# Layer ends of a float32 transformer on one core: weights of the next layer split ahead into free slots, VectorE and ScalarE in program order up to the end of the next layer's first group

## The chip, the cores and the metric

The kernel runs on one core of one Trainium2 chip. The metric is the device time of one launch in microseconds; it counts as changed when it moves by more than the measurement can tell. All operands are float32 in memory and all weights lie in HBM.

## The reference, cut to what matters

A forward pass over 512 positions of width 1024, two blocks of four layers in all, each layer a mixer and a gated FFN with a residual around each:

```python
def rms_norm(x, g):  # x / sqrt(mean(x*x) + eps) * g, over the 1024 channels
def first_block(x, ...):
    for layer in range(DEPTH):              # 2: retention, then attention with a shared K and V
        if layer < N_A_LAYERS:
            h = retention(rms_norm(x, a_norm_pre[i]), a_w_in[i], a_w_out[i])
            x = x + rms_norm(h, a_norm_post[i])
        else:
            kv = rms_norm(x, kv_norm) @ w_kv
            h = diff_attention(rms_norm(x, b_norm_pre[i]), k_sh, v_sh, b_w_q[i], ...)
            x = x + rms_norm(h, b_norm_post[i])
        h = conv_ffn(rms_norm(x, ffn_norm_pre[layer]), ffn_w_up[layer], ...)
        x = x + rms_norm(h, ffn_norm_post[layer])
    return x
```

The second block is a conformer convolution, an FFN, NSA attention and an FFN, its residuals without a norm behind the branch.

What matters here: in the first block the branch's output is normed before it is added, so a layer cannot begin before the sums over all 1024 channels of the branch's output are known. There are four such layer ends: retention to FFN 0, FFN 0 to shared K and V ("diff"), attention to FFN 1, FFN 1 to conformer.

## The kernel before, in words

Activations lie transposed: a row tile is 128 channels by 512 positions, eight of them make x. Matmul operands are pairs of a rounded high part and a low part, and each product is three matmuls (high·high, high·low, low·high; mm3, L250 to L255). Weights stream in chunks of eight 128x128 tiles (Stream): SyncE loads a chunk into one of four raw buffers (L92), ScalarE writes its high part (L106) and VectorE its low part (L107) into one of three split buffers. A chunk's split buffer is free again when TensorE has passed the chunk that lay there. All weights are taken in the order in which the program is traced, so the position of a take in the program decides when its chunk is split.

A planner orders each engine's instructions by their place in the program and by when it takes their inputs to be ready. Where the program asks for a manual schedule for an engine (in_order), the instructions that it traces there keep their program order on that engine.

A layer's last columns are `tail` (L326): they are computed in two halves of 256 positions, each weight being used twice, so that the sums of squares of the first half (Residual.sums, L289 by colsum) can be taken while the second half is still multiplied. From the sums come the scale per position (L305, L306 and the Newton steps L296 to L299) and its spread over 128 channels by two transposes into a bank (L312). In done, L337 adds the column to the branch's output, L339 squares it, L341 adds the square to the sums. Only TensorE is kept in program order, during the tail.

The next layer begins with a group of six columns (`group`, L409): the banks of six columns are open at once and each row tile of x is multiplied into all six as soon as it is ready. In group_halves the first three row tiles are taken in halves (L457), then row tiles 3 to 7 in full (outer, L473 and L474 with the high part of x, L477 with the low part). A row tile is made by Residual.apply (L202 multiplies the branch by the spread scale, once a half; L204 adds it to x), then its high part on ScalarE (L267) and its low part on VectorE (L268). For the group's own norm each row tile of x is squared on ScalarE (L276 the first, L279 the others) and added on VectorE (L280); the norm's scale is not needed before the columns are read out of their banks, so its sums (L289), Newton steps and spread (L312) stand behind the group. Row tiles 3 to 7 and the norm are left to the planner. Outside the four layer ends the same group is used without a residual (Prep.step).

In ffn, six columns (three gated pairs) come from the group; gated reads a pair out of its banks (L661, L665), convolves (L640, L642) and makes the next operand (L667, L670, L264, L265). The columns of the fourth pair are traced behind the three pairs. In diff, a few small instructions for lambda (L843 to L852) are traced ahead of the group; pq (L267, L268 again) prepares a second norm of the same x behind it.

## Time and profile before

| | |
|---|---|
| median of 3 runs | 2697.86 us (2697.57 to 2698.37) |
| the profiled execution | 2698.97 us |
| its span, first to last instruction | 2697.2 us |
| TensorE matmul busy | 2663.1 us (99%) |
| VectorE busy | 1679.4 us (62%) |
| ScalarE busy | 1200.1 us (44%) |
| mean granted TensorE clock | 0.997 |

In the rows below, a row of a timeline gives the start in us from the span's start, the duration in us, engine, line, operation, what it writes and reads, and in square brackets the idle time of the engine before it and what ended it. A row with x18 stands for that many instructions in a row. PE is TensorE, DVE VectorE, ACT ScalarE. Ends of matmuls are modelled and overlap the next start; starts are what to compare.

### The profile page before, as it was taken

Reading aid. Unit: us, or ns where it says so; the run is one execution under the profiler, and the core shown is the slowest. Engines: PE = TensorE matmul, PEld = TensorE weight load, DVE = VectorE, ACT = ScalarE, POOL = GpSimd, SP = SyncE. Lnnn points to the kernel's source line nnn. Section 1 sums busy time; section 2 is a strip of 40 time slices with the busy share of each in tenths; the row PEclk is TensorE's granted clock in tenths of the full one; section 3 lists DMA queues with packets and bytes.
Section 4 is the critical chain, followed back from the end, with each engine's and each line's share of the span. In section 5 each row is a group of like instructions: output and inputs, shape, how many; then the busy total and the mean of one; then the engine's idle time right before and its main releaser. Section 6 shows DMA issues by size and latency. Waiting matters only on the chain.

```text
span 2697.2 us, 35698 instructions
## 1 busy us (share of the span) xinstructions
PE 2663.1 (99%) x14187; PEld 2223.9 (82%) x14187; DVE 1679.4 (62%) x2777; ACT 1200.1 (44%) x1956; POOL 118.8 (4%) x125
## 2 busy tenths in 40 slices
PE   9999999999999999999999999999999999999999
PEld 8888888788888878788888588888887777888887
DVE  6545557836656687845748966445447788564453
ACT  5443434434445674533434244323347676442331
POOL 0000000000001100000003300000001111000000
PEclk9999999999999999999999999999999999999999
DMA  5223222323322112322323323223343101223322
GB/s 181 79 75 101 82 79 71 109 94 97 101 86 87 57 46 78 94 94 99 99 90 105 111 72 96 98 94 119 117 136 122 40 9 44 75 94 95 101 95 86
DMA packets 73256, 243.46 MB, mean 90 GB/s; under 512 B 9216, under 2 KB 12160, under 8 KB 73088
## 3 DMA queue, kind: packets, MB, share of 16 engines
q1 hardware_dynamic: 73088, 241.18, 28.1%
q8 instruction: 111, 1.82, 0.3%
q14 instruction: 57, 0.47, 0.1%
HBM read 229.63 MB, written 4.19 MB: 87 GB/s over the span
## 4 chain that ended last, share of the span: by engine, by line
PE 89%; DVE 7%; ACT 2%; issue 1%; POOL 0%; DMA 0%; SPq 0%; POOLq 0%; ACTq 0%; DVEq 0%
PE bank L253 23%; PE bank L255 23%; PE bank L254 23%; PE bank L473 3%; PE bank L474 3%; PE bank L477 3%; PE bank L770 2%; PE bank L457 2%; DVE bank L1079 1%; PE bank L1559 1%; PE bank L826 1%; PE bank L1068 1%; PE bank L289 1%; DVE w_spl L107 1%; DVE arena_f L642 1%
## 5 line engine op out<-in xcount | busy, mean ns | idle before, releaser
L253 PE MATMUL bank<-arena_r,w_spl 128*128 128x512 f32 (+1 forms) x2732 | 1059.5, 388 | 4.8 <-ACT w_spl L106 2.6
L254 PE MATMUL bank<-arena_r,w_spl 128*128 128x512 f32 (+1 forms) x2732 | 1052.3, 385 | 0.8 <-DVE arena_r L265 0.8
L255 PE MATMUL bank<-arena_r,w_spl 128*128 128x512 f32 (+1 forms) x2732 | 1049.4, 384 | 0.8 <-DVE w_spl L107 0.8
L106 ACT ACTIVATE w_spl<-w_raw 128x1024 fp32r<-128x1024 f32 (+1 forms) x424 | 448.4, 1058 | 728.9 <-PE bank L254 456.0
L107 DVE TENSOR_TENSOR w_spl<-w_raw,w_spl 128x1024 fp32r<-128x1024 f32 (+1 forms) x414 | 507.3, 1226 | 401.6 <-ACT w_spl L106 398.6
L253 PEld LDWEIGHTS bank<-arena_r,w_spl 128*128 128x128 f32 x2732 | 514.4, 188 | 108.9 <-ACT w_spl L106 4.8
L255 PEld LDWEIGHTS bank<-arena_r,w_spl 128*128 128x128 f32 x2732 | 514.0, 188 | 102.6 <-DVE w_spl L107 1.6
L254 PEld LDWEIGHTS bank<-arena_r,w_spl 128*128 128x128 f32 x2732 | 514.3, 188 | 98.4 <-issue 1.4
L642 DVE SCALAR_TENSOR_TENSOR arena_f<-arena_f,vec 128x510 f32<-128x510 f32 (+1 forms) x264 | 194.9, 747 | 3.4
L264 ACT ACTIVATE arena_r<-arena_f 128x512 fp32r<-128x512 f32 (+1 forms) x153 | 91.9, 610 | 189.8 <-DVE arena_f L670 152.4
L253 PE MATMUL bank<-w_spl,arena_r 128*128 128x256 f32 (+1 forms) x480 | 138.9, 290 | 2.1 <-ACT arena_r L1346 1.5
L665 DVE TENSOR_TENSOR arena_f<-bank,arena_f 128x512 f32<-128x512 f32 x88 | 60.7, 689 | 125.9 <-PE bank L255 125.9
L473 PE MATMUL bank<-arena_r,w_spl 128*128 128x512 f32 (+1 forms) x350 | 136.2, 391 | 2.2 <-ACT arena_r L264 1.9
L255 PE MATMUL bank<-w_spl,arena_r 128*128 128x256 f32 (+1 forms) x480 | 136.7, 286 | 0.1
L254 PE MATMUL bank<-w_spl,arena_r 128*128 128x256 f32 (+1 forms) x480 | 136.4, 284 | 0.0
L474 PE MATMUL bank<-arena_r,w_spl 128*128 128x512 f32 (+1 forms) x350 | 135.7, 389 | 0.0
L265 DVE TENSOR_TENSOR arena_r<-arena_f,arena_r 128x512 fp32r<-128x512 f32 (+1 forms) x153 | 100.6, 670 | 35.2 <-ACT arena_r L264 34.5
L790 ACT ACTIVATE arena_f<-bank,small 128x128 f32<-128x128 f32 (+3 forms) x192 | 99.7, 526 | 49.5 <-DVE small L787 44.4
L667 ACT ACTIVATE arena_f<-arena_f 128x512 f32<-128x512 f32 x88 | 55.5, 631 | 138.6 <-DVE arena_f L642 138.5
L640 ACT ACTIVATE arena_f<-arena_f,vec 128x512 f32<-128x512 f32 x132 | 106.1, 809 | 19.5 <-DVE arena_f L661 17.6
L661 DVE TENSOR_TENSOR arena_f<-bank,arena_f 128x512 f32<-128x512 f32 x88 | 60.5, 688 | 81.3 <-PE bank L255 72.9
L787 DVE TENSOR_REDUCE small<-bank 128x1 f32<-128x128 f32 (+3 forms) x192 | 86.6, 483 | 23.2 <-PE bank L775 22.5
(228 smaller groups left out, 2894.0 us busy)
## 6 DMA issues: line engine op xcount, KB each, us to landing
w_raw<-w SPq DMA_DIRECT2D x422, 512.0 KB, 3.5
arena_f<-tab SPq DMA_DIRECT2D x10, 256.0 KB, 3.2
arena_f<-x SPq DMA_DIRECT2D x8, 256.0 KB, 6.4
x_wait<-arena_f SPq DMA_DIRECT2D x8, 256.0 KB, 2.1
arena_f<-x_wait SPq DMA_DIRECT2D x8, 256.0 KB, 2.6
out<-arena_f SPq DMA_DIRECT2D x8, 256.0 KB, 2.2
arena_r<-arena_f SPq DMA_DIRECT2D x20, 64.0 KB, 2.0
arena_r<-arena_f SPq DMA_DIRECT2D x20, 63.9 KB, 2.0
```

The costliest lines, as they stand in the source:

```text
L106: self.nc.scalar.activation(hi, r, AF.Copy)
L107: (self.lo_engine or self.nc.vector).tensor_tensor(lo, r, hi, op=ALU.subtract)
L253: mm(out, a[0], b[0], start=start, stop=False, skip_group_check=skip)
L254: mm(out, a[0], b[1], start=False, stop=False, skip_group_check=skip)
L255: mm(out, a[1], b[0], start=False, stop=stop, skip_group_check=skip)
L264: self.nc.scalar.activation(h, src, AF.Copy)
L265: self.nc.vector.tensor_tensor(l, src, h, op=ALU.subtract)
L473: mm(b, w[0], hi[:, sl], start=(k == 0 and sl.start == 0), stop=False, skip_group_check=True)
L474: mm(b, w[1], hi[:, sl], start=False, stop=False, skip_group_check=True)
L640: nc.scalar.activation(c.a, u.a, AF.Identity, bias=self.v(cb, j), scale=self.v(cw, 2 * nj + j))
L642: nc.vector.scalar_tensor_tensor(c.a[:, d:], u.a[:, :S - d], self.v(cw, (2 - d) * nj + j), c.a[:, d:], op0=ALU.mult, op1=ALU.add)
L790: nc.scalar.activation(p.a[:, :n], outs[c], AF.Exp, bias=mx[:, c:c + 1], accum_out=sm[:, c:c + 1])
```

## The change

Five things are changed, all around the four layer ends except the last two.

1. Stream can put the split parts of a chunk into a run of four free slots of the operand arena (parts with park, release). In the tail chunks are split up to three chunks beyond the tail's own weights, before its second half begins; nothing of them is taken back until the columns that use them have been passed.
2. From the tail's second half to the end of the next group VectorE and ScalarE are in program order, and TensorE from the tail's start to the end of the group. The order is written out: half_high and half_low, high, sums and low are traced one by one; the last column's done is traced between the first row tile's high and low part.
3. The group's norm: the sums (colsum) and the Newton steps are traced ahead of the last row tile's products, the spread right behind them. This holds for the groups without a residual too.
4. In ffn two columns of the fourth pair are traced between the first three gated pairs.
5. In diff the lambda instructions are traced behind the group.

```diff
-    def parts(self, upto):
-        while self.split < min(upto, self.n):
+    def parts(self, upto, park=False):
+        while self.split < min(upto, self.n) and (self.ring or park):
             c = self.split
+            if self.ring:
+                i = self.ring.popleft()
+                self.home[c] = (i, self.spl[:, i, 0], self.spl[:, i, 1])
+            else:
+                s = self.arena.run(4)
+                w = [self.whole[:, s[h].i:s[h].i + 2].rearrange("p a n -> p (a n)") for h in (0, 2)]
+                self.home[c] = (s, *w)
...
+    def high(self):
         b, k = self.b, len(self.xs)
         p = (b.R.get(), b.R.get())
         if self.update is not None:
             self.update.apply(k, slice(0, S))
-        b.pair(b.x[k].a, b.v(self.g, k), [s.a for s in p])
+        b.nc.scalar.activation(p[0].a, b.x[k].a, AF.Copy, scale=b.v(self.g, k))
         self.xs.append(p)
+    def low(self):
+        b, k = self.b, len(self.xs) - 1
+        hi, lo = self.xs[k]
+        b.nc.vector.scalar_tensor_tensor(lo.a, b.x[k].a, b.v(self.g, k), hi.a, op0=ALU.mult, op1=ALU.subtract)
         if self.want:
             self.squares.append(k)
+    def sums(self, n=KD):
+        while n > 0 and self.squares:
+            self.acc = self.b.sumsq(self.acc, self.b.x[self.squares.popleft()].a)
+            n -= 1
...
     def tail(self, name, ns, xs, ks, hs):
...
+        res.region = self.in_order(mybir.EngineType.PE)
+        res.region.__enter__()
+        W.holding = True
+        ahead = (len(W.order) + len(ns) * len(ks) - 1) // CHUNK + 4
...
+        for half, sl in enumerate(HALVES):
+            if half == 1:
+                W.parts(ahead, True)
+                res.order = self.in_order(mybir.EngineType.DVE, mybir.EngineType.Activation)
+                res.order.__enter__()
...
+                if half == 1 and n == ns[-1]:
+                    res.last = lambda: done(b, n, sl)
...
     def group(self, name, ns, prep):
...
-        for k in range(first, KD):
-            prep.step()
+        up = prep.update
+        if up is not None:
+            self.group_halves(name, list(ns), 3, banks, prep)
+        for k in range(max(0, len(xs) - 1), KD):
+            if up is None:
+                prep.step()
+            elif k < KD - 1:
+                prep.high()
+                prep.sums(2)
+                prep.low()
+            if k == KD - 1:
+                prep.sums()
+                st = self.P.get()
+                self.colsum(st, [prep.acc])
+                prep.acc.free()
+                rs = self.rstd(st.a, 4, D, True)
             self.outer(name, ns, k, banks, xs[k])
-        while prep.squares:
-            prep.acc = self.sumsq(prep.acc, self.x[prep.squares.popleft()].a)
-        return banks
+        if up is not None:
+            up.order.__exit__(None, None, None)
+            up.region.__exit__(None, None, None)
+        self.spread(st, rs)
+        rb = self.F.get()
+        self.nc.scalar.activation(rb.a, st.a, AF.Copy)
+        st.free()
+        return banks, rb, rs
     def group_halves(self, name, ns, m, banks, prep):
...
         for half, sl in enumerate(HALVES):
             for k in range(m):
-                prep.half(k, sl)
-                W.after = self.last_hi.ins
+                if k == 0:
+                    prep.half_high(0, sl)
+                    if half == 0:
+                        res.last()
+                        prep.half_low(0, sl)
+                        res.rest()
+                        prep.half_high(1, sl)
+                    else:
+                        prep.half_high(1, sl)
+                        prep.half_low(0, sl)
+                elif k == 1:
+                    prep.half_high(2, sl)
+                    prep.half_low(1, sl)
+                    if half == 0:
+                        prep.half_low(2, sl)
+                        res.scale(1)
+                elif half == 1:
+                    prep.half_low(2, sl)
+                if half == 1 and k > 0:
+                    W.release(ws[k, ns[0]][0])
+                    W.parts(ws[k, ns[0]][0] + NSPL)
...
-        W.hold()
+        prep.high()
+        prep.low()
+        W.go_on()
...
-                banks = self.group(up, ns, pr)
-                st, rs = self.norm_cols(pr.acc, keep=True)
+                banks, rb, _ = self.group(up, ns, pr)
+                nxt = []
                 for q in range(first):
                     ps.append(gated(banks[2 * q], banks[2 * q + 1], q))
-            elif j >= first:
+                    if q < 2:
+                        nxt.append(self.col(up, first + q * NF, xs))
+                ps.append(gated(*nxt, first))
+            elif j > first:
```

## Rows read from the trace of the kernel before

**Rows 1.** Page, part 1: busy us (share of the span) xinstructions.
```profile
PE 2663.1 (99%) x14187; PEld 2223.9 (82%) x14187; DVE 1679.4 (62%) x2777; ACT 1200.1 (44%) x1956; POOL 118.8 (4%) x125
```
**Rows 2.** Waits of TensorE: engine line, waited for: us, times, longest us.
```profile
PE bank L457 <- ACT arena_r L267: 5.8, 4, 1.4
PE bank L253 <- ACT w_spl L106: 3.1, 4, 0.9
PE bank L312 <- DVE small L299: 2.7, 3, 1.7
...
PE bank L312 <- DVE keep L299: 1.2, 2, 0.9
...
PE bank L477 <- DVE arena_r L268: 0.7, 1, 0.7
```
**Rows 3.** Timeline of TensorE where the shared K and V stage begins.
```profile
785.11 0.38 PE L312 MATMUL bank<-cst,small 128*128 128x128 f32 x2
...
785.91 0.28 PE L255 MATMUL bank<-arena_r,w_spl 128*128 128x256 f32 x1
787.64 2.42 PE L457 MATMUL bank<-arena_r,w_spl 128*128 128x256 f32 x18 [1.45 <-ACT arena_r L267]
789.90 0.95 PE L289 MATMUL bank<-vec,arena_f 128*128 128x1 f32 x8
790.71 0.84 PE L457 MATMUL bank<-arena_r,w_spl 128*128 128x256 f32 x5
```
**Rows 4.** Timeline of VectorE and of ScalarE at the same place.
```profile
785.52 0.75 DVE L202 TENSOR_TENSOR arena_f<-arena_f,bank 128x256 f32<-128x256 f32 x2
...
786.57 0.88 DVE L204 SCALAR_TENSOR_TENSOR arena_f<-arena_f,vec 128x256 f32<-128x256 f32 x2
...
787.08 0.51 ACT L267 ACTIVATE arena_r<-arena_f,vec 128x256 fp32r<-128x256 f32 x1
```
**Rows 5.** Timeline of TensorE at the end of retention.
```profile
415.39 0.43 PE L312 MATMUL bank<-cst,small 128*128 128x128 f32 x2 [0.55 <-DVE small L299]
```
**Rows 6.** VectorE by line and form, 793 to 817.5: xcount, busy us, mean ns, idle before.
```profile
L268 DVE SCALAR_TENSOR_TENSOR arena_r<-arena_f,vec,arena_r 128x512 fp32r<-128x512 f32 x10 | 7.2, 745 | 0.0
L107 DVE TENSOR_TENSOR w_spl<-w_raw,w_spl 128x1024 fp32r<-128x1024 f32 x4 | 4.9, 1222 | 0.4 <-ACT w_spl L106 0.4
L280 DVE TENSOR_TENSOR arena_f<-arena_f 128x512 f32<-128x512 f32 x7 | 4.8, 681 | 0.0
L204 DVE SCALAR_TENSOR_TENSOR arena_f<-arena_f,vec 128x512 f32<-128x512 f32 x5 | 3.7, 744 | 0.0
L202 DVE TENSOR_TENSOR arena_f<-arena_f,bank 128x256 f32<-128x256 f32 x9 | 3.5, 413 | 0.1
```
**Rows 7.** ScalarE by line and form in the same stretch.
```profile
L267 ACT ACTIVATE arena_r<-arena_f,vec 128x512 fp32r<-128x512 f32 x13 | 8.8, 709 | 0.0
L106 ACT ACTIVATE w_spl<-w_raw 128x1024 fp32r<-128x1024 f32 x5 | 5.3, 1060 | 4.9 <-issue 3.9 <-ACT arena_r L267 0.9
L279 ACT ACTIVATE arena_f<-arena_f 128x512 f32<-128x512 f32 x7 | 4.3, 616 | 0.0
```
**Rows 8.** Timeline of TensorE: first matmuls of two row tiles that follow each other.
```profile
801.79 0.40 PE L473 MATMUL bank<-arena_r,w_spl 128*128 128x512 f32 x1
...
805.89 0.39 PE L473 MATMUL bank<-arena_r,w_spl 128*128 128x512 f32 x1
```
**Rows 9.** Timeline of VectorE in the group of FFN 0.
```profile
444.52 1.23 DVE L107 TENSOR_TENSOR w_spl<-w_raw,w_spl 128x1024 fp32r<-128x1024 f32 x1 [0.71 <-ACT w_spl L106]
...
449.96 1.23 DVE L107 TENSOR_TENSOR w_spl<-w_raw,w_spl 128x1024 fp32r<-128x1024 f32 x1 [2.95 <-ACT w_spl L106]
```
**Rows 10.** Timelines of VectorE and TensorE behind the group of FFN 0.
```profile
472.72 1.22 DVE L107 TENSOR_TENSOR w_spl<-w_raw,w_spl 128x1024 fp32r<-128x1024 f32 x1
...
474.00 0.50 PE L255 MATMUL bank<-arena_r,w_spl 128*128 128x512 f32 x1 [0.38 <-DVE w_spl L107]
```
**Rows 11.** Stretch behind the end of retention: length, PE, PEld, DVE, ACT, POOL, PEclk, DMA, GB/s.
```profile
417.98:421.66 3.68, 3.68 (x19) 3.68 (x20) 2.94 (x6) 1.70 (x3) 0.00 (x0) 0.56 0.13 20
```

## What the change should do to the time, predicted from the trace of before

> **What bounds the kernel now.** I read the page's busy shares first: TensorE is busy for 99% of the span, so nearly everything that this change can win is idle time of TensorE, and anything that makes TensorE wait is lost in full, since nothing behind it has slack [rows 1]. Then the waits of TensorE, to see where the rest lies. The layer ends show up as L457, four times and 1.45 µs each, and L312 on "small", three times, of which the longest (1.7) belongs to a norm that the change does not touch; L477 and L312 on "keep" are in the conformer's group and, for 0.4 of its 1.2, the NSA group; L253 on "w_spl" is mostly weights that come late after the two first FFN groups [rows 2]. Then the timeline at a layer end (the shared-KV stage's): the two transposes that spread the first half's scale start at 785.11, call that moment S; the last matmul of the old layer starts at 785.91, and the first of the new one only at 787.64, so 1.6 µs are lost [rows 3], while VectorE does four instructions that the first row tile does not need between the two that it does [rows 4].
>
> **The switch itself.** In program order the chain from S is: L202 begins 0.41 later, 0.41 long, L204 0.48, L267 0.51, with hops of 0.03 to 0.05, so the first L457 can start at S+1.92 instead of S+2.53 [rows 3, 4]. That is 0.61 a layer end, 2.4 for four. The wait of L312 for the small scale [rows 5] comes from a weight split that VectorE runs ahead of it; in two ends it is 0.55 and 0.5. With the weights of three chunks split ahead into free slots during the last columns, VectorE has only half-width adds there (of L202's size, 0.41), nothing holds the scale up, and both waits go: 1.05, and 0.3 for the two restarts of the pipeline, 1.4. The splits moved ahead are three per end, 1.06 on ScalarE and 1.22 on VectorE each [rows 6, 7]; they lie beside old-layer columns in which VectorE is half idle, so I cost them at nothing; without that cover one of them would put back 1.2. Their loads on SP's queue go out earlier by the same three chunks, with four raw buffers still ahead; no wait of TensorE in the trace is on a load, so I cost this at nothing too, and at most one load (3.5 µs, the page's median) if it is not so.
>
> **What follows the switch.** Here is the cost. From the second half of the last columns to the end of the group VectorE and ScalarE now run exactly in program order. On the ruler S, TensorE needs, without waits, 1.92 + 6 × 2.16 for the six half row tiles (18 matmuls at 0.12, as 18 take 2.42 with the last one's drain) + 0.8 for L289 [rows 3] + 0.1 for L312 (an estimate: its pair's 0.38 less the drain) = S+15.8 until the first full row tile, and 4.10 for each of those (801.79 to 805.89) [rows 8]. It wants the sums of squares, now ahead of the last row tile, at S+15.8+4×4.10 = S+32.2.
>
> VectorE's queue: the second spread starts at S+7.05 (1.92 + 2×2.16 + 0.8), so the second halves begin 0.41 later; three half tiles are 3×1.19 (L202, L204, L268 in half width) and a wait of 0.5 for ScalarE, S+11.5. A weight chunk stands next: ScalarE's part ends at S+12.0, VectorE's at S+13.25. Row tile 3 is L202 twice, L204, wait for L267, L268: 0.34+0.45+0.75+0.74+0.75, so its high part is there at S+15.45 (in time for 15.8) and its low part at 16.2; behind another chunk's low part VectorE is free at S+17.6. From there a row tile is, in the order written (high, two sums, low, then the outer product's weight chunk): 0.34+0.45+0.75 for L202, L202, L204; then VectorE stands before its add until ScalarE has done L267 and the square behind it, 0.71+0.62 less the overlap, 1.30; the two adds 0.61 each, L268 0.67, the chunk's L107 1.15 (starts follow each other 0.08 closer than the durations in [rows 6, 7]). That makes 5.88 with two adds and 5.27 with one, against TensorE's 4.10. Row tile 4 has two squares to wait for (1.83 with L267), one add and no chunk: 4.65. Then 5.88, 5.88, 5.27 and a last add 0.65: 22.3, so the sums are done at about S+39.9 and not at 32.2. TensorE loses 7.7 a layer end, part of it on the way in row tiles 5 and 6, most of it before L289, and it stands there in program order with the whole last row tile behind it. Four ends: 30.8.
>
> That VectorE stands still with ready work behind it is seen before the change: at 444.52 it had waited 0.71 for ScalarE's half of a chunk, and the low part of a row tile and the last add came after it; but there the planner had spread the work so that the add was over at 447.0 and VectorE then idle for 2.95 [rows 9]. The Trainium skill (TensorE: Matmul & The Clock Gate, section "Architectural detail") says that ScalarE's and VectorE's queues are strict FIFO. By that rule the 7.7 stand; a queue that let ready work pass would leave the 1.2 of the rival below. The trace agrees with the rule in the row just named.
>
> **The other parts.** The norm's chain behind the group is hidden by the last row tile: 0.67 and 0.86 of idle in the conformer, with 0.3 of restarts 1.8; 0.4 in NSA [rows 2]. In the FFN groups it was already hidden by columns, so nothing there. After the two first FFN groups VectorE works off three gated pairs before the weights that stand behind them: the low part that TensorE waits for at 474.00 was split at 472.72 [rows 10]; with the hesitation around it and the 0.9 at 480.20 (a share of L253's 3.1 in [rows 2]) that is 2.1 a group. Two columns traced between the pairs bring their weight chunks forward, and the pairs no longer wait for the norm behind the group; the fourth pair is traced ahead of the next chunks, which takes some of it back. I take 1.5 of 2.1, twice 1.5 = 3.0; ends 0 and 4.2. The lambda block (six small VectorE and ScalarE instructions and one table load) goes behind the group; it was early and unneeded, nothing, at worst one load of a table. The groups without a residual only change the place of L289 and L312, whose inputs are ready long before: nothing.
>
> The clock: after the idle at 415.39 and 416.5 the granted clock of the next 3.68 µs was 0.56, that is mostly at 1.2 instead of 2.4 GHz, and the same 18 matmuls take 2.26 at 787.64 [rows 3, 5, 11]. Without the idle this 1.4 goes.
>
> **Sum.** −2.4 −1.4 −1.8 −0.4 −3.0 −1.4 + 30.8 = +20.4. The profiled execution took 2698.97 (span 2697.2); its sum is 2719.4. It lies 1.1 above the median 2697.86, so 2718.
>
> **Rivals.** *VectorE keeps pace* (faster). If its waits for ScalarE are filled, its own work from S+17.6 is 4×2.02 for the four row tiles, 7×0.61 adds, 3×1.15 chunks, 15.8: S+33.4, and TensorE loses 1.2 or, with any head start, nothing. Then the gains of 10.4 stand against 0 to 4.8: 2687 to 2692, say 2690. It decides itself where a row tile of VectorE takes 4.1. For it: the work was done in that time before [rows 9]. Against it: the written order. Chance 0.22.
> *Only the high part is waited for.* If the squares are done beforehand (0.6 less in four tiles) and the last chunk's low part falls behind the last add (1.15), the loss is 4.1 an end, 16.4 in all: +6, 2704. Chance 0.13.
> *Slower still.* Each layer end now has one idle of some 4.7 µs. If the clock falls after it as at 417.98, 1.4 is added once or twice an end: 2724 to 2729; other work that the planner lets into the region (eight row tiles of the second norm in the shared-KV stage, 0.67 of VectorE each) costs the same kind, up to 5. The Trainium skill (the same page, section "What's actually happening") says that an idle TensorE falls to half clock by itself. In this trace it did so after the idle at 415 and did not after the 1.45 at 787. Chance 0.12.
> *It does not do what it says:* should the region not hold VectorE and ScalarE to program order at all, the planner's order stays and with it the first rival's time; it is counted there.
>
> **How the numbers follow.** Forecast 0.53, 2711 to 2724; rivals 0.22, 0.13, 0.12. A measurement here tells 0.2%, 5.4 µs, from no change: faster is below 2692.5, slower above 2703.3. Faster 0.21; same 0.09 (the low side of the second rival and the top of the first); slower 0.70. The range goes from 2690, in the middle of the first rival, to 2728; about 0.15 is left out. The forecast's own range is 2711 to 2724, from the unknown share of the FFN weights and ±1.5 an end.
>
> **What would show it.** Right: at each layer end the first L457-like matmul 1.9 after the spread instead of 2.5; no wait for the small scale; then a wait of TensorE at the norm's sums of 4 to 5 µs, released by VectorE's add, and short waits on the row tiles' high and low parts in the two tiles before; VectorE's waits for ScalarE's squares some 1.3 each. Wrong: no wait at the sums, or one under 1.5; waits on weights in the parked slots or on loads, which would be a cause I have at nothing; or the FFN's waits for weights unchanged.

## The result and the profile after

The changed kernel takes 2723.39 us (median of four runs, 2721.82 to 2723.72), the kernel before 2698.11 (four runs, 2697.57 to 2698.91): ratio 1.0092, 95% interval 1.008 to 1.0104, so 25 us slower. The profiled execution took 2723.72 with a span of 2721.9.

First the page's busy line (busy us, share of the span, instructions), which answers to [rows 1]. The work is the same; TensorE has 8 us more busy time and 17 us more idle time.

```profile
PE 2671.1 (98%) x14187; PEld 2225.2 (82%) x14187; DVE 1685.0 (62%) x2777; ACT 1199.8 (44%) x1955; POOL 117.1 (4%) x125
```

Then the waits of TensorE (engine line, waited for: us in all, times, longest), the counterpart of [rows 2].

```profile
PE bank L575 <- DVE arena_r L210: 8.7, 7, 2.4
PE bank L302 <- DVE w_spl L118: 7.6, 2, 3.8
PE bank L571 <- ACT arena_r L203: 3.8, 8, 0.8
PE bank L555 <- ACT arena_r L188: 3.5, 4, 0.9
PE bank L300 <- ACT arena_f L503: 2.3, 3, 1.2
PE bank L300 <- DVE arena_f L1218: 2.0, 1, 2.0
```

L555 is the first half row tile (L457 before): 0.87 at each layer end instead of 1.45, as forecast. The wait for the small scale at two layer ends is gone. New are the waits of L575 for a row tile's low part (L210), of L571 for its high part (L203; one of the eight, 0.8, stands in the first group of retention), and two of 3.8 for a weight chunk's low part (L118). In none of the four layer-end groups is there a wait at the norm's column sums, L336.

Where the 25 us arise can be read off TensorE alone: both traces hold 14187 of its instructions, so the start of the n-th in one can be set against the n-th in the other. Where both have done the same work, the difference is the lag. (Worked out from the starts in the traces; columns of the table below: the time in the kernel before, and the lag of after.)

```
place                                            before    after
last columns of retention                         410.2     +1.0
first half row tile, FFN 0                        418.0     -0.4
first columns behind that group                   461.4     +2.4
behind the gated pairs of FFN 0                   492.6     +6.3
first half row tile, shared K and V               787.9     +5.7
behind that group                                 832.2    +13.3
first half row tile, FFN 1                       1048.1    +11.7
behind that group                                1089.5    +16.0
behind the gated pairs of FFN 1                  1116.8    +19.8
first half row tile, conformer                   1416.0    +19.2
behind that group                                1454.5    +23.8
behind its gated columns                         1467.6    +26.5
last instruction                                 2693.2    +24.7
```

The switches (from the last columns to the first half row tile) win 1.4, 0.6, 1.3 and 0.6; the lag ahead of the third is 13.0, and the two larger gains hold 0.7 each for the small scale's wait. The four groups lose 2.8, 7.6, 4.3 and 4.6, the first after winning 1.5 because the clock does not fall there. The stretches behind three of them lose another 3.9, 3.8 and 2.7.

The K and V group loses most. The planner put the low parts of the second norm of the same x (L210 again, eight of 0.75) into the ordered stretch, seven of them ahead of the last add, and a row tile of VectorE takes 6.58 there:

```profile
818.79 1.49 DVE L327 TENSOR_TENSOR arena_f<-arena_f 128x512 f32<-128x512 f32 x2 [1.31 <-ACT arena_f L326]
...
822.65 0.75 DVE L210 SCALAR_TENSOR_TENSOR arena_r<-arena_f,vec,arena_r 128x512 fp32r<-128x512 f32 x1
...
825.37 1.49 DVE L327 TENSOR_TENSOR arena_f<-arena_f 128x512 f32<-128x512 f32 x2 [1.31 <-ACT arena_f L326]
```

Both losses, in the group and behind it, have one place each in the timelines of FFN 0. TensorE first (start, length, line, operands, count, idle before and what ended it):

```profile
415.66 0.38 PE L359 MATMUL bank<-cst,small 128*128 128x128 f32 x2
...
417.61 0.61 PE L555 MATMUL bank<-arena_r 128*128 128x256 f32 x3 [0.87 <-ACT arena_r L188]
...
443.13 0.74 PE L575 MATMUL bank<-arena_r,w_spl 128*128 128x512 f32 x2 [1.51 <-DVE arena_r L210]
...
449.17 1.19 PE L575 MATMUL bank<-arena_r,w_spl 128*128 128x512 f32 x4 [0.60 <-DVE arena_r L210]
...
451.57 0.39 PE L300 MATMUL bank<-arena_r,w_spl 128*128 128x512 f32 x1
...
456.33 0.95 PE L336 MATMUL bank<-vec,arena_f 128*128 128x1 f32 x8
457.14 0.49 PE L571 MATMUL bank<-arena_r,w_spl 128*128 128x512 f32 x1
...
485.30 0.68 PE L302 MATMUL bank<-arena_r,w_spl 128*128 128x512 f32 x1 [3.81 <-DVE w_spl L118]
```

And VectorE at the same place:

```profile
440.92 1.49 DVE L327 TENSOR_TENSOR arena_f<-arena_f 128x512 f32<-128x512 f32 x2 [1.31 <-ACT arena_f L326]
...
446.96 1.49 DVE L327 TENSOR_TENSOR arena_f<-arena_f 128x512 f32<-128x512 f32 x2 [1.31 <-ACT arena_f L326]
...
455.42 0.69 DVE L327 TENSOR_TENSOR arena_f<-arena_f 128x512 f32<-128x512 f32 x1
...
463.85 0.68 DVE L754 TENSOR_TENSOR arena_f<-bank,arena_f 128x512 f32<-128x512 f32 x1
...
484.03 1.22 DVE L118 TENSOR_TENSOR w_spl<-w_raw,w_spl 128x1024 fp32r<-128x1024 f32 x1
```

VectorE stands 1.31 before its adds in row tiles 5 to 7, the tiles follow each other at 6.04 (440.92 to 446.96), and the last add ends at 456.11. With S at 415.66 that is S+40.4; the forecast had S+39.9. But TensorE does not stand there: from 451.57 to 456.33 it does 21 matmuls of the fourth pair's first column, which the planner put into the ordered stretch ahead of L336. What it loses it loses earlier, on low and high parts that come at VectorE's pace, and later: the late sums make the scale late, so the gated pairs start at 463.85 instead of 459.45 in the kernel before; VectorE works them off, the fourth among them, before it splits the chunk that TensorE needs next, and begins its low part at 484.03, with TensorE waiting.

The clock's side, in stretches (us; PE, PEld, DVE, ACT and POOL busy, instructions; granted clock; DMA share; GB/s). Behind FFN 0's switch it is at 2.4 GHz throughout, where [rows 11] showed 0.56. It fell to 1.2 GHz for most of some 3.5 us in four other places, each at the end of an idle of 2.0 to 3.8 us that the change had brought, or within 1.3 us of it.

```profile
415.60:450.00 34.40, 31.20 (x194) 26.93 (x194) 25.70 (x51) 13.85 (x23) 0.00 (x0) 1.00 0.16 47
...
485.30:488.90 3.60, 3.60 (x9) 2.84 (x10) 3.60 (x6) 1.22 (x2) 0.00 (x0) 0.53 0.58 181
1127.20:1130.70 3.50, 3.47 (x8) 2.77 (x9) 3.50 (x6) 1.10 (x2) 0.00 (x0) 0.52 0.61 171
1461.90:1465.10 3.20, 3.20 (x8) 2.55 (x9) 3.16 (x4) 0.00 (x0) 0.85 (x1) 0.50 0.06 20
1485.40:1489.20 3.80, 3.80 (x12) 2.95 (x11) 3.80 (x5) 2.37 (x4) 1.69 (x1) 0.55 0.69 177
```

### The profile page after: what moved, and what is told of

It reads as the page before. It is cut to its first block, busy times and chain, and to the rows that moved or that the text cites. A ratio compares the mean times of both kernels' runs of the same rounds, so it can differ in the third digit from the quotient of the medians.

```text
span 2721.9 us, 35688 instructions
## 1 busy us (share of the span) xinstructions
PE 2671.1 (98%) x14187; PEld 2225.2 (82%) x14187; DVE 1685.0 (62%) x2777; ACT 1199.8 (44%) x1955; POOL 117.1 (4%) x125
## 4 chain that ended last, share of the span: by engine, by line
PE 88%; DVE 7%; ACT 3%; issue 1%; POOL 0%; DMA 0%; SPq 0%; POOLq 0%; DVEq 0%; ACTq 0%
PE bank L300 24%; PE bank L302 24%; PE bank L301 24%; PE bank L575 2%; PE bank L571 2%; PE bank L572 2%; PE bank L862 2%; PE bank L1635 1%; PE bank L918 1%; DVE w_spl L118 1%; PE bank L1154 1%; PE bank L336 1%; DVE arena_f L251 1%; DVE bank L1165 1%; DVE arena_f L249 1%
## 5 line engine op out<-in xcount | busy, mean ns | idle before, releaser
L117 ACT ACTIVATE w_spl<-w_raw 128x1024 fp32r<-128x1024 f32 (+1 forms) x412 | 435.5, 1057 | 705.2 <-PE bank L301 446.8
L118 DVE TENSOR_TENSOR w_spl<-w_raw,w_spl 128x1024 fp32r<-128x1024 f32 (+1 forms) x402 | 493.1, 1227 | 373.3 <-ACT w_spl L117 370.0
L571 PE MATMUL bank<-arena_r,w_spl 128*128 128x512 f32 (+1 forms) x326 | 129.6, 399 | 6.0 <-ACT arena_r L203 3.2
```

What stands on the lines that cost most here:

```text
L117: self.nc.scalar.activation(hi, r, AF.Copy)
L118: (self.lo_engine or self.nc.vector).tensor_tensor(lo, r, hi, op=ALU.subtract)
L571: mm(b, w[0], hi[:, sl], start=(k == 0 and sl.start == 0), stop=False, skip_group_check=True)
```

## The experiments

Theory Q is the forecast's: VectorE and ScalarE, held to the written order through row tiles 3 to 7, set TensorE's pace and make the sums late. Its rivals: the columns moved between the gated pairs, the chunks parked ahead, or the place of the norm. All kernels below are the changed kernel with one edit, unless another base is named. Each was timed beside the kernel before, on the same chip. The table of lags at the end puts them side by side.

### Let the order go at the end of the half row tiles

```diff
         if up is not None:
-            up.order.__exit__(None, None, None)
             up.region.__exit__(None, None, None)
...
         prep.low()
         W.go_on()
+        res.order.__exit__(None, None, None)
```

> After, but VectorE and ScalarE leave program order at the end of the half row tiles; TensorE keeps it to the end of the group. By the count of TensorE's instructions the changed kernel falls behind by 3.7, 7.5, 4.3 and 4.4 us inside its four layer-end groups, 19.9 in all. Theory Q (the written order of VectorE and ScalarE in row tiles 3 to 7 is the cause): 14 to 20 of these come back, 2703 to 2709, and the 1.3 us waits of VectorE for squares go. Rival (the work itself, the weights split ahead or TensorE's order are the cause): within 3 us of 2723. The wait for a low part behind the FFN groups (3.98 and 3.82) stays at 2 to 4 by both.

Measured: 2693.27 (10 runs), ratio to before 0.998, interval 0.997 to 0.9989. That is 30 us below the changed kernel, more than all it had lost, and more than the 14 to 20 expected: the waits behind the FFN groups, which the expectation left at 2 to 4, went too. So both losses hang on the order of VectorE and ScalarE in row tiles 4 to 7 (row tile 3's high and low part are still written ahead of the place where the order is let go). With the waits went the clock's four new falls; one, at 866.91, came instead. One thing was given back. Timelines of ScalarE and TensorE at the end of retention:

```profile
415.91 1.06 ACT L117 ACTIVATE w_spl<-w_raw 128x1024 fp32r<-128x1024 f32 x1 [0.70 <-PE bank L301]
...
417.42 0.86 PE L555 MATMUL bank<-arena_r 128*128 128x256 f32 x5 [1.48 <-ACT arena_r L188]
```

A chunk that is traced behind the ordered stretch was placed in the middle of it, ScalarE's part ahead of the first half tile's high part, and the switch costs 1.48 again. The ordered stretch fixes the order of what is traced in it; it does not keep other work out.

### The norm behind the last row tile

```diff
-            if k == KD - 1:
-                prep.sums()
...
-                rs = self.rstd(st.a, 4, D, True)
             self.outer(name, ns, k, banks, xs[k])
+        prep.sums()
...
+        rs = self.rstd(st.a, 4, D, True)
```

> After, with the sums of squares, their column sums and the scale behind the last row tile again, in every group. The recorded forecast put most of the 7.7 us an end before the column sums, with the last row tile stuck behind them; by that, the last row tile (4.1) now covers more than half: 12 to 16 faster, 2707 to 2711. Theory F (columns of the next work that the planner put ahead of the column sums fill that wait already, and the loss is in the row tiles): within 4 us of 2723, rather slower by 0 to 3, as the conformer's and the NSA group's waits for the norm (0.7, 0.9 and 0.4 before) come back.

Measured: 2715.42, ratio 1.0061, 1.0046 to 1.0076: 8 faster than the changed kernel, between the two. The groups themselves lose 2.6, 6.7, 3.6 and 4.6, nearly as before; what goes is the loss behind the FFN groups, -0.2 each instead of +3.9 and +3.8, while 2.8 are lost between the conformer and the end, where after had won 1.8. TensorE's wait for the norm is back in the conformer's and the NSA group:

```profile
PE bank L359 <- DVE keep L346: 1.2, 2, 0.9
```

That covers 1.2 of these. Another 1.8 is a longer wait for the conformer's gated columns, 3.7 instead of 1.9 (the line is L1215 in after):

```profile
PE bank L300 <- DVE arena_f L1214: 3.7, 1, 3.7
```

VectorE behind FFN 0's group:

```profile
462.04 0.69 DVE L753 TENSOR_TENSOR arena_f<-bank,arena_f 128x512 f32<-128x512 f32 x1 [2.08 <-ACT arena_f L502]
...
480.50 1.22 DVE L118 TENSOR_TENSOR w_spl<-w_raw,w_spl 128x1024 fp32r<-128x1024 f32 x1
```

In the changed kernel the spread of the scale stands behind a last row tile that stands behind the late sums. With the last row tile in front, the spread and the pairs come 1.8 earlier (462.04 instead of 463.85), the late chunk 3.5 earlier. So the place of the sums costs, but not as the forecast had it: no wait at L336, but a late spread.

### The fourth pair's columns back behind the three pairs

```diff
-                nxt = []
                 for q in range(first):
                     ps.append(gated(banks[2 * q], banks[2 * q + 1], q))
-                    if q < 2:
-                        nxt.append(self.col(up, first + q * NF, xs))
-                ps.append(gated(*nxt, first))
-            elif j > first:
+            elif j >= first:
```

> After, with the fourth gated pair's columns traced behind the three pairs, as before the change (both FFN). Theory P (the fourth pair, traced ahead of the next chunk, makes the chunk's low part late): the two waits of 3.98 and 3.82 and the half clock behind each (1.9) go, 11.6, and the 1.85 that the columns brought forward had won comes back twice: 2715, 2712 to 2719. Rival (the pairs start 4.4 us late because the norm's sums are late, the place of the columns is not the cause): the waits stay above 2.5 each, 2720 to 2726.

Measured: 2719.28, ratio 1.0076, 1.0061 to 1.0091, 4 faster, just between the two ranges (2712 to 2719 and 2720 to 2726), half of the 8 expected. The wait for the chunk's low part, in the waits of TensorE of this run, has halved and not gone:

```profile
PE bank L302 <- DVE w_spl L118: 3.5, 2, 1.7
```

So the columns' place is about half of that wait, and the lateness of the pairs the other half. The next run shows which of them comes first.

### Order let go, and the columns back

Both edits above (the first and the third).

> Both edits of the two runs beside it: order released at the end of the half row tiles, and the fourth pair's columns back. If queue and columns are two separate causes, their gains add: 14 to 20 and 8, 2695 to 2702, near the kernel before. If the late sums cause both, the time is that of the release alone, within 2 us.

Measured: 2692.36, ratio 0.9978, 0.9969 to 0.9988: the time of the release alone, within 1. The gains do not add. With the sums in time the columns' place is worth nothing, for or against; the late sums cause both.

### Low part ahead of the sums

```diff
                 prep.high()
-                prep.sums(2)
                 prep.low()
+                prep.sums(2)
```

> After, with the low part of each row tile written ahead of the two sums instead of behind them; program order stays. Theory Q as counted in the forecast (VectorE's row tile is 5.9 us because it stands 1.3 before its adds): now it stands 0.7 before the low part and 0.5 before the adds, 1.2 in all, so the sums come hardly earlier, but each low part comes 1.9 earlier. TensorE's pace in the row tiles is still VectorE's: 2 to 6 faster, 2717 to 2721. Rival (only the lateness of the low part costs, 8.7 us of waits and their restarts): 9 to 14 faster, 2709 to 2714.

Measured: 2702.92, ratio 1.0015, 1.0006 to 1.0024: 20 us faster by moving one line, far outside both expectations. VectorE in FFN 0's group:

```profile
439.54 0.75 DVE L210 SCALAR_TENSOR_TENSOR arena_r<-arena_f,vec,arena_r 128x512 fp32r<-128x512 f32 x1 [0.79 <-ACT arena_r L203]
440.21 1.48 DVE L327 TENSOR_TENSOR arena_f<-arena_f 128x512 f32<-128x512 f32 x2
...
445.06 0.75 DVE L210 SCALAR_TENSOR_TENSOR arena_r<-arena_f,vec,arena_r 128x512 fp32r<-128x512 f32 x1 [0.79 <-ACT arena_r L203]
```

The row tile falls from 6.04 to 5.52 (439.54 to 445.06), because the squares now end while VectorE does the low part: one wait of 0.79 instead of 1.31. The expectation had two waits, 1.2 in all, and left out that the last square can be summed one tile earlier, ahead of the last chunk. So the sums end at 452.7, 3.4 before the changed kernel's, and that counts in the group and again behind the pairs: behind FFN 0's pairs this kernel loses nothing (-0.7 before and behind them in the table), the changed one 3.9. TensorE's waits for low parts (8.7 in the changed kernel) are gone too, those for high parts rise from 3.8 to 7.3, and of the clock's four new falls one is left, in FFN 1. What the earlier low parts are worth by themselves and what the earlier sums, this run does not separate.

### Adds one row tile behind their squares

```diff
                 prep.high()
-                prep.sums(2)
+                prep.adds()
                 prep.low()
+                prep.square(2)
             if k == KD - 1:
+                prep.adds()
                 prep.sums()
...
```

(`square` issues ScalarE's squares, `adds` VectorE's adds of the squares issued a tile earlier.)

> After, still in program order to the end of the group, but each add of a square is written one row tile behind its square: VectorE does the two halves, the step into x, the adds of the tile before, the low part, the chunk; ScalarE the high part, the squares, the chunk. Nothing then stands for ScalarE: a row tile is 1.54 + 1.22 + 0.67 + 1.15 = 4.6 us on VectorE against 4.1 on TensorE. Theory Q1 (the wait for the squares, as written, is what is too long; program order by itself is not): the row tiles lose 2 an end instead of 4 to 7, the sums come 4 earlier and with them the gated pairs: 15 to 25 faster, 2698 to 2708. Theory Q2 (any fixed order of VectorE and ScalarE costs it): within 5 of 2723.

Measured: 2710.27, ratio 1.0039, 1.0025 to 1.0053, 13 faster: between the two. The wait before the adds is gone, and another stands in its place. VectorE:

```profile
439.86 1.23 DVE L118 TENSOR_TENSOR w_spl<-w_raw,w_spl 128x1024 fp32r<-128x1024 f32 x1 [1.24 <-ACT w_spl L117]
...
445.32 1.23 DVE L118 TENSOR_TENSOR w_spl<-w_raw,w_spl 128x1024 fp32r<-128x1024 f32 x1 [0.79 <-ACT w_spl L117]
```

Now ScalarE has the high part and both squares to do before its half of the chunk, and VectorE stands for that. The row tile is 5.46 (439.86 to 445.32), not the 4.7 that is left of it without that wait.

### The adds on GpSimd

```diff
-        nc.vector.tensor_tensor(acc.a, acc.a, t.a, op=ALU.add)
+        (eng or nc.vector).tensor_tensor(acc.a, acc.a, t.a, op=ALU.add)
```

(with GpSimd as `eng` in the layer-end groups.)

> After, order as changed, but the adds of the squares in the layer-end groups run on GpSimd instead of VectorE (0.61 each on VectorE; GpSimd's 128x512 add took 1.16 in the kernel before). VectorE then does the two halves, the step into x, the low part and the chunk, with one wait of 0.8 for the high part: 3.0 us a row tile without a chunk, 4.2 with one, against 4.1 on TensorE. Theory Q (TensorE goes at VectorE's pace through row tiles 3 to 7, and every late sum makes the pairs behind it late): the stalls of the row tiles go, the sums come at about S+35 instead of S+40.4, 15 to 22 faster, 2702 to 2708. Rival (the fixed order hurts whatever VectorE's time): within 6 of 2723.

Measured: 2712.58, ratio 1.0055, 1.0038 to 1.0072, 11 faster, outside both expectations. VectorE, with two fewer adds in each row tile:

```profile
438.73 0.75 DVE L210 SCALAR_TENSOR_TENSOR arena_r<-arena_f,vec,arena_r 128x512 fp32r<-128x512 f32 x1 [0.79 <-ACT arena_r L203]
440.72 1.23 DVE L118 TENSOR_TENSOR w_spl<-w_raw,w_spl 128x1024 fp32r<-128x1024 f32 x1 [1.24 <-ACT w_spl L117]
...
442.64 1.00 DVE L251 SCALAR_TENSOR_TENSOR arena_f<-arena_f,vec 128x512 f32<-128x512 f32 x1
444.43 0.75 DVE L210 SCALAR_TENSOR_TENSOR arena_r<-arena_f,vec,arena_r 128x512 fp32r<-128x512 f32 x1 [0.79 <-ACT arena_r L203]
```

The row tile is still 5.70 (438.73 to 444.43), with 2.0 of it waits. This is what the expectation counted wrong: a fixed order makes the row tile a chain, VectorE's step into x, ScalarE's high part, squares and chunk, VectorE's chunk, and only then the next step into x. Taking work from VectorE shortens it little (0.34 for two adds), because VectorE then waits for ScalarE, and its step into x (L251) takes 1.00 instead of 0.75 beside GpSimd's adds. Theory Q stands in the form that the written chain across the two engines is too long; in the form that VectorE has too much to do it falls.

### The release, with outside chunks held behind the half tiles

On the base of the release: ScalarE's part of a chunk traced behind the ordered stretch is bound behind the last half tile's high part, as the kernel before had it.

```diff
-                self.nc.scalar.activation(hi, r, AF.Copy)
+                with self.tc.issue_after(self.after) if self.after else nullcontext():
+                    self.nc.scalar.activation(hi, r, AF.Copy)
...
         W.go_on()
         res.order.__exit__(None, None, None)
+        W.after = prep.last_hi.ins
```

> The release at the end of the half row tiles once more; there a chunk traced behind the ordered stretch slipped into it (VectorE split it at 417.00, ahead of the first half tile's low part) and TensorE stood 1.48 at the switch again. Here ScalarE's part of such chunks may not run before the last half tile's high part. Theory: the switch comes 0.6 earlier in four ends, 2.4, and one half clock of 1.4 at 418 more or less: 2689 to 2691.5 against 2693.3 of the release, faster than the kernel before by 0.25 to 0.35%. Rival (the chunk is then late in the row tiles and costs there what the switch wins): 2693 to 2695.

Measured: 2691.15 (six runs, 2688.50 to 2692.12), ratio to the kernel before 0.9969, 0.9958 to 0.9981, as the theory had it. The first of the waits of TensorE is the switch at its shorter price (L558 and L189 are L555 and L188 of after):

```profile
PE bank L558 <- ACT arena_r L189: 3.5, 4, 0.9
```

Its row tiles in FFN 0 start at 431.74, 435.85 and 439.93, the 4.1 of [rows 8], with no wait. The same kernel, run once more under another label:

> The release with the outside chunk held behind the half tiles, once more and with nothing changed, so that its profile and its time stand beside the other two runs of this call on one chip: 2691 by its first measurement (2688.5 to 2692.1).

Measured: 2691.91.

### The release, with the norm behind the last row tile

> The release at the end of the half row tiles, with the sums of squares, column sums and scale behind the last row tile. By the forecast's term for the conformer's and the NSA group's norm (1.8 and 0.4), which the sums ahead of the last row tile should hide: 2.2 slower than the release, 2695.5. Rival (the planner hides the norm with other work as soon as the order is free): within 0.7 of 2693.3.

Measured: 2698.32, ratio 0.9997, 0.9988 to 1.0006, 5.0 above the release by the medians (4.2 when each is set against the kernel before, timed beside it), 2.8 by the two profiled spans. The expected 2.2 had no share in the FFN groups, and that is where most of it is. TensorE behind FFN 0's group, and the stretch from there (columns as above):

```profile
478.63 0.78 PE L302 MATMUL bank<-arena_r,w_spl 128*128 128x512 f32 x1 [1.78 <-DVE w_spl L118]
...
478.60:482.10 3.50, 3.47 (x8) 2.80 (x9) 3.50 (x6) 1.18 (x2) 0.00 (x0) 0.51 0.49 162
```

A later norm makes the pairs later and the chunk behind them late; and the matmuls behind that wait run at the lower clock (granted clock 0.51 over 3.5 us).

### No chunks parked ahead

On the base with outside chunks held behind: one chunk is split during the second half of the last columns, one between the half row tiles, into the ring's slots as they come free.

```diff
-        ahead = (len(W.order) + len(ns) * len(ks) - 1) // CHUNK + 4
+        ahead = (len(W.order) + len(ns) * len(ks) - 1) // CHUNK + 1
...
                         W.release(ws[n, k][0])
+                        W.parts(ahead + 3)
```

(and `W.parts` again behind the third half tile's high part.)

> The release with the outside chunk held behind the half tiles, but no chunk is split ahead into free slots of the arena: one chunk is split during the second half of the last columns and one between the half row tiles, as the ring's slots come free. The forecast's term: the waits for the small scale come back in two ends (1.05 and 0.3) and one chunk of 1.2 in the ordered stretch delays the second spread or a low part by 0.5 to 1.2 an end: 3 to 6 slower, 2694 to 2697. Rival (parking is without effect, the order at the switch does it all): within 1 of 2691.

Measured: 2711.62, ratio 1.0048, 1.0033 to 1.0063, 20 slower than its base instead of 3 to 6. In FFN 0 the switch is 0.8 later (418.36 against 417.59) and the second spread another 1.5, more than the 0.5 to 1.2 expected for it; most of the rest is a chunk that now waits for its slot. ScalarE and TensorE in FFN 0's group, and the stretch from there:

```profile
431.66 1.06 ACT L118 ACTIVATE w_spl<-w_raw 128x1024 fp32r<-128x1024 f32 x1 [1.89 <-PE bank L562]
...
436.44 0.50 PE L578 MATMUL bank<-arena_r,w_spl 128*128 128x512 f32 x1 [2.18 <-ACT arena_r L204]
...
436.40:440.20 3.80, 3.76 (x10) 2.95 (x11) 3.80 (x6) 2.59 (x4) 0.00 (x0) 0.56 0.16 59
```

(line numbers are one to seven above those of after: L578 is the high part's matmul of a row tile, L571 there.) ScalarE cannot split the chunk before the half row tiles have read the old one; row tile 3's high part, written behind it, comes 2.2 late, and TensorE goes on at a granted clock of 0.56. The clock falls once in each of the four groups, in the base in none. So on this base, and with these two places for the chunks, parking is worth 20 us. Other places were not tried, and the longest of these waits stands where row tile 3 is still in written order.

### Outside chunks held behind, and the low part ahead of the sums

> The release with the outside chunk held behind the half tiles, and there too the low part of each row tile written ahead of the two sums. In program order this edit won 20 us. Theory (it won them because the queues had to follow the written order; the planner, free in row tiles 4 to 7, sees the same dependencies either way): within 1.5 of 2691.2. Rival (the written order also sets the planner's choice, and sums that are traced later come later): 3 to 5 slower or faster, 2686 to 2688 or 2694 to 2696.

Measured: 2691.09 (eight runs), ratio 0.9971, 0.996 to 0.9982. The edit that won 20 us in program order is worth nothing once the planner orders the row tiles.

### Side by side

Lag of TensorE behind the kernel before, as above:

```
                       FFN 0                K and V        FFN 1                conformer
             switch group pairs    switch group   switch group pairs   switch group gated    end
after          -0.4  +2.4  +6.3      +5.7 +13.3    +11.7 +16.0 +19.8    +19.2 +23.8 +26.5  +24.7
release        -0.6  -2.1  -3.6      -3.6  -3.2     -2.7  -2.7  -4.2     -4.2  -4.4  -5.1   -3.6
norm behind    -1.3  +1.3  +1.1      +0.5  +7.2     +5.6  +9.2  +9.0     +8.4 +13.0 +13.5  +16.3
columns back   -0.7  +2.0  +3.6      +3.0 +10.7    +10.5 +14.8 +16.3    +15.7 +20.2 +21.4  +20.8
low first      -0.6  -0.7  -0.7      -1.3  +3.0     +1.3  +2.8  +4.4     +3.8  +5.5  +5.5   +3.9
GpSimd adds    -1.2  +2.1  +1.4      +0.8  +7.0     +5.4  +8.5  +7.8     +7.2 +11.7 +12.3  +11.7
chunk behind   -0.4  -1.9  -3.4      -4.0  -3.6     -5.2  -5.2  -6.8     -7.4  -7.2  -7.9   -8.4
no parking     +0.4  +4.5  +3.0      +2.6  +8.3     +7.8 +13.5 +11.9    +11.5 +16.5 +15.9  +13.9
```

## Why the prediction was right, and where its steps were not

The sign, the size and the cause were right: 2718 against 2723.4, inside 2711 to 2724, and the cause is the written order of VectorE and ScalarE, since letting it go returns 30 us. But the size is in part luck. By the lags, with the forecast's terms sorted by place:

```
                                     forecast   measured
start of retention                        0.0       +1.0
the four switches                        -3.8       -3.9
the four groups, clock at 418 within    +29.4      +19.3
behind three of the groups               -4.8      +10.4
elsewhere                                -0.4       -2.1
sum                                     +20.4      +24.7
```

The groups lose 10 less than forecast and the stretches behind them 15 more; of two large errors only their difference, the 5 us by which the forecast was low, shows in the time. Step by step:

**The switch** (-2.4): S+1.95 (415.66 to 417.61) against the S+1.92 of the forecast, 0.58 won at each end. **The small scale's waits** (-1.4): gone in the two ends. **The clock at 418** (-1.4): that drop is gone. **The norm in the conformer and in NSA** (-1.8, -0.4): its waits are gone, but in the conformer TensorE now stands 2.0 for the gated columns (L1218), a wait that is not there once the order is let go.

**VectorE's queue** (+30.8): the queue itself was forecast closely. In FFN 0 its row tiles 4 to 7 take 4.64, 6.04, 6.04 and 5.26 (from 433.44 to the last add at 455.42) against 4.65, 5.88, 5.88 and 5.27, and the sums came at S+40.4 against S+39.9. What TensorE loses by it was forecast 10 too large: it is 20.8 in the four groups, without the 1.5 that the clock gives back in the first. The step "it stands there in program order with the whole last row tile behind it" failed: program order on TensorE did not keep the planner from putting columns ahead of the column sums, 4.8 to 5.4 us of them in each group, and those were work, not a wait. The forecast's own list of signs has "no wait at the sums" under wrong, and for this step it was wrong. The loss sits in the row tiles and, unforeseen, behind the pairs. In the K and V group it is larger by what the rival "slower still" names, the second norm's low parts in the region.

**The FFN's weights** (-3.0): wrong in sign, +7.7, and for a reason that the sum held the pieces of: late sums make the pairs late, and the pairs stand ahead of the chunk. In the release the same stretches win 1.5 each (-2.1 to -3.6, -2.7 to -4.2), 3.0 as forecast. But they win it with the columns back as well; it is the norm ahead of the last row tile that wins it. "In the FFN groups it was already hidden by columns, so nothing there" was the mistake.

**The splits ahead, at nothing:** right, and their worth was never counted: 20 us against the same kernel without parking (in the two places tried), where "1.2 put back" was the bound.

**Nothing at the start of retention:** the lag there is 1.0 in after, of which 0.8 is a wait for a row tile's high part at 12.64. In the other kernels it is 0.0 to 2.4, and it need not be the change: the release with outside chunks held behind, run twice, has 1.0 in one execution and 0.4 in the other. The two kernels with the norm behind the last row tile, which undo the change to this group too, both have 0.0; whether that is more than scatter stays open.

**The clock's new falls** were left to the rival "slower still", and its mechanism is what happened, four times in all and not at the sums. A fall costs some 1.7 (an estimate: 3.5 us at little over half), 6.8 together, against the 1.5 of the one that went. Its bottom end, 2724, was nearly met.

The rival "VectorE keeps pace" gave 2687 to 2692 for the case that its row tile takes 4.1: with the order let go that is 2693.3 and 2691.2. The rival "only the high part is waited for" gave 2704 for squares done beforehand and the last chunk behind the last add. Low part ahead of the sums makes nearly that order, and took 2702.9; but its groups lose 7.4 by the table, 8.9 without the clock's 1.5, where the rival has 16.4, so that the time agrees is luck in part.

## What to carry to other kernels

Fix an engine's order by hand only as far as the stretch that needs it: here the six half tiles, where it won 0.6 an end, and not the row tiles behind them, where two engines that hand work to each other within one tile turn into one chain. Count such a chain as a chain, across both engines and in the written order; moving work to a third engine shortens it only if the work lies on it. When something becomes late, follow it past the first consumer: the late sums cost nothing at the matmul that reads them in these groups, and 10.4 us behind three of the four.

## What the hardware showed

Two things were not expected. The granted clock fell to 1.2 GHz behind single idles of very different length: 3.81 at 485.30 of after, 2.18 at 436.44 without parking, and, in the run with GpSimd's adds, 1.41 at 454.32, with a granted clock of 0.68 over the 5.3 us from there:

```profile
454.32 1.05 PE L336 MATMUL bank<-vec,arena_f 128*128 128x1 f32 x8 [1.41 <-POOL arena_f L327]
...
454.40:459.70 5.30, 5.30 (x21) 4.35 (x22) 0.74 (x5) 0.27 (x1) 0.00 (x0) 0.68 0.26 87
```

Behind the 1.51 at 443.13 of after and the 1.48 at 417.42 of the release it did not fall. The Trainium skill (TensorE: Matmul & The Clock Gate, section "What's actually happening") has the idle engine fall by itself; that agrees, but which idle of 1.4 to 1.5 us is followed by a fall cannot be told from these runs.

And VectorE and GpSimd slow each other. GpSimd's rows in that run, and one of VectorE's:

```profile
436.09 1.30 POOL L327 TENSOR_TENSOR arena_f<-arena_f 128x512 f32<-128x512 f32 x1 [418.31 <-ACT arena_f L326]
439.36 3.74 POOL L327 TENSOR_TENSOR arena_f<-arena_f 128x512 f32<-128x512 f32 x2 [1.97 <-ACT arena_f L326]
...
436.45 1.49 DVE L251 SCALAR_TENSOR_TENSOR arena_f<-arena_f,vec 128x512 f32<-128x512 f32 x1
```

An add that began first took 1.30, and VectorE's L251, which reads two operands from SBUF and began 0.36 behind it, took 1.49 instead of 0.75. Two adds, the second beside VectorE's chunk split, took 3.74 instead of 2.60, and the L251 that met the end of it took 1.00; the pair of L249, which reads one of its operands from a bank, kept its 0.75. The Trainium skill (SBUF — State Buffer, section "Summary: rules for kernel authors") says that a VectorE instruction with two inputs in SBUF and a GpSimd instruction that reads SBUF block each other, the second to issue waiting for the first. The rows agree: 0.74 added on VectorE behind an add, 1.14 on GpSimd beside a split of 1.23.

The changed kernel meets this in the conformer's group, where GpSimd prepares the convolution (L1131):

```profile
1458.81 2.37 DVE L327 TENSOR_TENSOR arena_f<-arena_f 128x512 f32<-128x512 f32 x2 [1.31 <-ACT arena_f L326]
...
1461.77 2.06 DVE L118 TENSOR_TENSOR w_spl<-w_raw,w_spl 128x1024 fp32r<-128x1024 f32 x1
...
1459.59 1.05 POOL L1131 TENSOR_TENSOR arena_f<-arena_f 128x512 f32<-128x512 f32 x1 [5.59 <-DVE arena_f L327]
1461.26 1.49 POOL L1131 TENSOR_TENSOR arena_f<-arena_f 128x512 f32<-128x512 f32 x1 [0.63 <-DVE arena_f L327]
```

The two adds take 2.37 instead of 1.49, the chunk's low part 2.06 instead of 1.22, and the row tile 7.78 instead of 6.04. TensorE's longest wait for a low part (2.38, at 1461.90) and one of the four falls of the clock stand there.
